# A hybrid decoder layer on one core: 1/rms multiplications two per pooled tile, output-weight pieces in the attention branch, low parts of merged tiles two behind

## The chip, the cores and the metric

The kernel runs on one core of a Trainium2 chip. The metric is the device time of one execution in microseconds, the median of the runs taken; lower is better. Five engines work side by side, each through its own queue in program order: TensorE (PE in the profile; its weight loads are PEld), VectorE (DVE), ScalarE (ACT), GpSimd (POOL) and SyncE (SP), which here only issues transfers. They wait for each other through semaphores.

## The reference

A layer for 256 tokens of width 1024: two token mixers side by side, gated and summed, then a gated feed-forward part with a short convolution. Everything is float32.

```python
h = rmsnorm(x, norm_mix_g)
q, k, v, u_pool, gate_logits = split(h @ w_in)
attn = moba_attention(rope(rmsnorm(q)), rope(rmsnorm(k)), v)      # 8 heads of 64, one causal block
pooled = multiscale_pool_mixer(u_pool, w_pool, pool_scale)        # trailing means of 2, 4, 8, 16
gates = sigmoid(gate_logits + b_gate)                             # two branches of 1024
mixed = gates[0] * (attn @ w_branch_attn) + gates[1] * (pooled @ w_branch_pool)
x = x + mixed @ w_out
h2 = rmsnorm(x, norm_ffn_g)
gate, val = split(causal_depthwise_conv(h2 @ w_up, conv_w, conv_b))
return x + (silu(gate) * val) @ w_down
```

## The kernel before

Activations lie with features on the 128 partitions and the 256 tokens along the free axis, so a feature tile is 128x256. Every float32 product is made of three matmuls (`mm3`, lines 99 to 105): each operand is split into a rounded high part (`high`, line 91, on ScalarE) and the rest as a low part (`low`, line 95 or 97, on VectorE), and high x high, high x low and low x high are summed in PSUM. TensorE takes three matmuls of 256 columns for each 128x128 block of weights.

Weights come in chunks of 128x2048 floats in the order of `order` (line 108): q, k, v, pool inputs, gates, pool maps, two chunks `bp` (pooled branch), two `ba` (attention branch), four `o` (output), then up and down chunks. Each passes four stages: a load on SP into one of four raw buffers, a high part on ScalarE and a low part on VectorE, in two pieces of 1024 columns each, and its use by TensorE. The splitting runs ahead of the use: every call of `ahead()` (line 199) takes the next high piece and the next low piece in order. Three rules limit it. The low piece lags one behind the high one (`STAGGER`). A high piece is not begun while its chunk is four or more ahead of the oldest chunk in use (`WBUFS`); that call then does nothing for it. When a chunk's last low piece is issued, `loads()` issues the load of the chunk four later into the raw buffer that it frees. So the place of an `ahead()` call in the program sets the place of one 128x1024 operation in the queue of ScalarE and one in that of VectorE, and of a load in SP's.

Every engine keeps its program order; the last lines (933 to 939) tie each instruction to the one before it on its engine.

The stage that the change touches has two loops of eight tiles, each tile twelve matmuls into one of four PSUM banks of the pool `mm`.

The pooled branch (lines 721 to 740): tile j of the pooled map, evacuated by a multiplication with its sigmoid gate (line 738; line 728 for tiles 4 and 5, where the attention values of all heads are also multiplied out in PSUM, weighed on VectorE at line 644, and split into the tiles `heads`). Six attention gates were copied out of PSUM earlier without their factor 1/rms (`plain`, line 704); they get it here (line 740), one a tile in tiles 0 to 5. ScalarE takes one sigmoid a tile (`sigmoids`, line 656), of the attention gates from tile 2 on. There is one `ahead()` in each tile.

The attention branch (lines 746 to 758): tile j is evacuated by a multiplication with its gate (line 753, VectorE), GpSimd adds the gated pooled tile (line 754), ScalarE rounds the sum to `mh` (line 755), VectorE makes the rest `ml` (line 757). The low part of tile j − 1 is issued in tile j, that of tile 7 behind the loop. `ahead()` is called in tiles 1 and 3 and behind the loop.

The output stage (lines 797 to 810) multiplies `mh` and `ml` with the output weights. For its first chunk it takes inputs 0 to 6 of its first tile, 0 to 6 of its second, and then input 7 of both.

Of the kernel before, what the change touches and what calls it, by code (L numbers as in the profile page):

```python
# [10 lines left out]
ALU = mybir.AluOpType  # L11
# [6 lines left out]
KD = D // P  # L18
# [38 lines left out]
VALUES = 4  # L57
# [13 lines left out]
def hybrid_layer_kernel(ctx: ExitStack, tc: tile.TileContext, xq_d, xtok_d, par_d, wkv_d, wpg_d,  # L71
                        wpool_d, wba_d, wbp_d, wout_d, wup_d, wdn_d, out_d):
    nc = tc.nc
# [16 lines left out]
    def high(hi, src, scale=1.0):  # L90
        nc.scalar.activation(hi, src, AF.Copy, scale=scale)  # L91

    def low(lo, hi, src, scale=None):
        if scale is None:
            nc.vector.tensor_tensor(lo, src, hi.bitcast(F32), ALU.subtract)  # L95
        else:
            nc.vector.scalar_tensor_tensor(lo, src, scale, hi.bitcast(F32), ALU.mult, ALU.subtract)
# [66 lines left out]
    def next_high():  # L164
        if at[0] < len(pieces):
            c, sl, first, _ = pieces[at[0]]
            if c - oldest() >= WBUFS:
                return
            at[0] += 1
            if first:  # L170
                moving = order[c][0] in "qkv"
                place = MOVING if moving else 0
                his[c] = whi_p.tile([P, CH + P], F32R, tag="whi", name=f"hi_{order[c][0]}{c}")[:, place:]
                place = MOVING if moving else FAR
                los[c] = wlo_p.tile([P, CH + P], F32R, tag="wlo", name=f"lo_{order[c][0]}{c}")[:, place:]
            high(his[c][:, sl], raw(c, sl))

    def next_low(eager=False):
        if at[1] < at[0] - STAGGER or at[0] == len(pieces) > at[1] or (at[1] < at[0] and eager):
            c, sl, _, last = pieces[at[1]]  # L180
            at[1] += 1
            low(los[c][:, sl], his[c][:, sl], raw(c, sl))
            if last:
                split.add(c)
                loads()
# [13 lines left out]
    def ahead(upto=0):  # L199

        next_high()
        next_low()
        if at[1] - sum(p[0] < used[0] for p in pieces) < upto:
            next_high()
            next_low()

    def chunk(name):
        c = used[0]
        used[0] += 1
        spent.update(i for i in range(c) if order[i][0] != "dn")  # L210
        assert order[c][0] == name and all(p[0] != c or name == "dn" and p[3] for p in pieces[at[1]:]), (name, order[c][0])
        return his[c], los[c]
# [63 lines left out]
    R1 = const.tile([P, S], F32, name="R1")  # L276
# [158 lines left out]
    def tick():  # L435
        clock[0] += 1
        for fn, args in due.pop(clock[0], []):
            fn(*args)
# [80 lines left out]
    def gate(n):  # L519
        return gates[:, n // 2, n % 2, :]  # L520
# [96 lines left out]
    def values(hps):  # L617

        po = ps2.tile([P, 2, 512], F32, tag="ps2", name=f"ps_o{hps[0]}")
        for i, hp in enumerate(hps):  # L620
            for b in range(2):
                for j in range(2):
                    h = 2 * hp + j
                    out = po[j * DH:(j + 1) * DH, i, 0:S].rearrange("p (a t r) -> p a t r", a=4, r=32)
                    nc.tensor.matmul(out[:, :, b:2, :], vn[:, b, h * DH:(h + 1) * DH],
                                     soft[hp][:, :, 3 * j + 2 * b:3 * j + b + 2, :], start=b == 0, stop=b == 1)
        return po
# [10 lines left out]
    def rounded(hps, po):  # L638
        if not heads:
            both = act.tile([P, 2, KA, S], F32R, tag="at", name="heads")  # L640
            heads.extend(both[:, i] for i in range(2))
        for i, hp in enumerate(hps):
            v = weighed(hp)
            nc.vector.tensor_tensor(v, po[:, i, 0:S].rearrange("p (a t r) -> p a t r", a=4, r=32), v, ALU.mult)
            high(tokens(heads[0], hp), natural(hp))

    def rests(hps):
        for hp in hps:
            low(tokens(heads[1], hp), tokens(heads[0], hp), natural(hp))
# [3 lines left out]
    def sigmoids(n):  # L653
        for _ in range(min(n, len(waiting))):
            f = waiting.pop(0)
            nc.scalar.activation(gate(f), gate(f), AF.Sigmoid, bias=par[:, C_BG + f:C_BG + f + 1])
# [19 lines left out]
    plain = []  # L676
    for n in range(2 * KD):
# [23 lines left out]
        f = 2 * GATES[b] + c  # L701
# [11 lines left out]
    def branch(src, oph, opl, j, w):  # L713
        hi, lo = w
        ps = bank(f"ps_b{src}{j}")
        for k in range(4):
            sl = slice(k * 512 + (j % 4) * P, k * 512 + (j % 4 + 1) * P)
            mm3(ps[:, 0:S], (hi[:, sl], lo[:, sl]), (oph[:, k, :], opl[:, k, :]), k == 0, k == 3)
        return ps

    for j in range(KD):
        if j % 4 == 0:
            w = chunk("bp")
        ps = branch("p", poolh, pooll, j, w)
        if j == VALUES:
            pos = [(hps, values(hps)) for hps in ((0, 1), (2, 3))]
        if j in (VALUES, VALUES + 1):
            nc.vector.tensor_tensor(gate(KD + j), ps[:, 0:S], gate(KD + j), ALU.mult)
            for hps, po in pos:
                rounded(hps, po) if j == VALUES else rests(hps)  # L730
        if j % 2 == 1:
            tick()
            ahead()
        if j in (0, 2, 4, 6):
            ahead()
        sigmoids(1)
        if j not in (VALUES, VALUES + 1):
            nc.vector.tensor_tensor(gate(KD + j), ps[:, 0:S], gate(KD + j), ALU.mult)
        if j < len(plain):
            nc.vector.tensor_tensor(gate(plain[j]), gate(plain[j]), R1, ALU.mult)  # L740
    mixer.close()
    tmp = ctx.enter_context(tc.tile_pool(name="ffn", bufs=2))
    mh = act.tile([P, KD, S], F32R, tag="qk", name="mh")
    ml = act.tile([P, KD, S], F32R, tag="v", name="ml")
    pend = []
    for j in range(KD):
        if j % 4 == 0:
            w = chunk("ba")
        ps = branch("a", heads[0], heads[1], j, w)
        sigmoids(1)  # L750
        if j in (1, 3):
            ahead()
        nc.vector.tensor_tensor(gate(j), ps[:, 0:S], gate(j), ALU.mult)
        nc.gpsimd.tensor_tensor(gate(j), gate(j), gate(KD + j), ALU.add)
        high(mh[:, j, :], gate(j))
        if j:
            low(ml[:, j - 1, :], mh[:, j - 1, :], gate(j - 1))
    low(ml[:, KD - 1, :], mh[:, KD - 1, :], gate(KD - 1))
    ahead()


# [243 lines left out]
```

## Time and profile before

| | us |
|---|---|
| median of 3 runs | 329.03 |
| lowest, highest | 328.9, 333.66 |
| profiled execution | 328.88 |
| its span, first to last instruction | 327.1 |
| mean granted TensorE clock | 1.00 |

The span was also cut into stages. Each row below is one stretch, in us from the span's start, with its length, each engine's busy time and (in brackets) instructions, the granted clock, the DMA share and GB/s. The first is the end of the gates, the second the pooled branch with the attention values, the third the attention branch, the fourth and fifth the output stage.

```profile
92.00:97.00 5.00, 5.00 (x47) 5.00 (x46) 4.26 (x6) 4.97 (x9) 0.00 (x0) 1.00 1.08 282
97.00:111.00 14.00, 14.00 (x132) 13.12 (x131) 11.61 (x25) 9.24 (x18) 0.00 (x0) 1.00 0.98 341
111.00:122.00 11.00, 11.00 (x99) 11.00 (x98) 8.68 (x18) 5.56 (x11) 5.11 (x6) 1.00 0.45 177
122.00:133.50 11.50, 11.50 (x104) 11.50 (x103) 8.29 (x14) 8.18 (x13) 2.67 (x4) 1.00 0.38 135
133.50:144.50 11.00, 11.00 (x100) 11.00 (x99) 8.51 (x14) 7.24 (x13) 3.10 (x4) 1.00 0.60 235
```

The order of the columns is PE, PEld, DVE, ACT, POOL. A timeline row gives the start and the duration in us, the engine, the line of the program, the operation and its output and inputs by the program's names (`xq` holds the gates as well as the input); in square brackets stands the idle time of the engine ahead of it and what ended that. A duration runs to the end of the pipeline: the next instruction of the same engine can start a little before it. A matmul record lasts 0.28 us although the next one starts after 0.113.

### The profile page before, as it was taken

To read this page: it belongs to the slowest core of one execution; us is meant where nothing else is said; L and a number is where in the kernel's file an instruction comes from. 1 tells how busy PE (TensorE), PEld (TensorE's weight loads), DVE (VectorE), ACT (ScalarE), POOL (GpSimd) and SP (SyncE) were. 2 spreads that over 40 slices of the span, in tenths; PEclk is the share of its full clock that TensorE was granted. 3 is DMA by queue.
4 is the path that set the end of the run, shared out by engine and by line. 5 is a ranking of instruction groups with operands and counts; after the bars stand their busy time and mean duration, and the time that the engine had idled before them with its cause. 6 is when DMAs were issued, how large, how long until landed. Compare 5 with 4: busy or idle time off the path is not lost.

```text
span 327.1 us, 6769 instructions
## 1 busy us (share of the span) xinstructions
PE 322.7 (99%) x2708; PEld 316.1 (97%) x2708; DVE 259.3 (79%) x447; ACT 201.8 (62%) x329; POOL 71.5 (22%) x89
## 2 busy tenths in 40 slices
PE   8999999999999999999999999999999999999995
PEld 8888899999999999999999999999999999999995
DVE  4839989999988966879997978686868686868834
ACT  5768518675994657669675647474747474746520
POOL 1006690000000151230421221212121212121330
PEclk9999999999999999999999999999999999999999
DMA  7999799947799833635527455464646464643003
GB/s 263 420 415 236 200 373 299 310 141 280 260 284 336 318 128 127 254 137 178 208 100 288 178 208 212 174 217 172 217 169 215 172 219 167 222 164 130 0 2 128
DMA packets 16542, 69.72 MB, mean 213 GB/s; under 512 B 2176, under 2 KB 7040, under 8 KB 9856
## 3 DMA queue, kind: packets, MB, share of 16 engines
q1 hardware_dynamic: 16096, 69.17, 60.1%
q8 instruction: 21, 0.34, 0.4%
q10 hardware_dynamic: 416, 0.13, 0.2%
q14 instruction: 9, 0.07, 0.1%
HBM read 65.61 MB, written 3.69 MB: 212 GB/s over the span
## 4 chain that ended last, share of the span: by engine, by line
PE 99%; DVE 0%; issue 0%
PE ps_up L105 12%; PE ps_up L103 12%; PE ps_up L104 12%; PE ps_d L867 6%; PE ps_d L865 6%; PE ps_d L866 6%; PE ps_g L103 5%; PE ps_g L105 4%; PE ps_g L104 4%; PE ps_q L333 4%; PE ps_k L333 3%; PE ps_v L333 3%; PE ps_out L103 2%; PE ps_out L105 2%; PE ps_out L104 2%; PE ps_warm L248 1%
## 5 line engine op out<-in xcount | busy, mean ns | idle before, releaser
L105 PE MATMUL ps_up<-hhi,lo_up 128*128 128x256 f32 x352 | 97.2, 276 | 0.0
L103 PE MATMUL ps_up<-hhi,hi_up 128*128 128x256 f32 x352 | 97.2, 276 | 0.0
L104 PE MATMUL ps_up<-hlo,hi_up 128*128 128x256 f32 x352 | 97.2, 276 | 0.0
L104 PEld LDWEIGHTS ps_up<-hlo,hi_up 128*128 128x128 f32 x352 | 66.1, 188 | 0.0
L105 PEld LDWEIGHTS ps_up<-hhi,lo_up 128*128 128x128 f32 x352 | 66.1, 188 | 0.0
L103 PEld LDWEIGHTS ps_up<-hhi,hi_up 128*128 128x128 f32 x352 | 66.1, 188 | 0.0
L95 DVE TENSOR_TENSOR lo_up<-raw_up,hi_up 128x1024 fp32r<-128x1024 f32 x44 | 54.7, 1261 | 7.3 <-ACT hi_up L91 7.3
L865 PE MATMUL ps_d<-ah,hi_dn 128*128 128x256 f32 x176 | 48.6, 276 | 0.0
L866 PE MATMUL ps_d<-al,hi_dn 128*128 128x256 f32 x176 | 48.6, 276 | 0.0
L867 PE MATMUL ps_d<-ah,lo_dn 128*128 128x256 f32 x176 | 48.6, 276 | 0.0
L91 ACT ACTIVATE hi_up<-raw_up 128x1024 fp32r<-128x1024 f32 x44 | 44.1, 1046 | 0.0
L847 POOL TENSOR_TENSOR c_v<-c_g,c_v 128x256 f32<-128x256 f32 x22 | 16.3, 739 | 121.4 <-DVE c_v L830 121.4
L91 ACT ACTIVATE ah<-c_v 128x256 fp32r<-128x256 f32 x22 | 9.2, 418 | 45.6 <-POOL c_v L847 45.6
L103 PE MATMUL ps_g<-xhi,hi_g 128*128 128x256 f32 x128 | 35.6, 278 | 0.0
L105 PE MATMUL ps_g<-xhi,lo_g 128*128 128x256 f32 x128 | 35.4, 276 | 0.0
L104 PE MATMUL ps_g<-xlo,hi_g 128*128 128x256 f32 x128 | 35.4, 276 | 0.0
L865 PEld LDWEIGHTS ps_d<-ah,hi_dn 128*128 128x128 f32 x176 | 33.0, 188 | 0.0
L866 PEld LDWEIGHTS ps_d<-al,hi_dn 128*128 128x128 f32 x176 | 33.0, 188 | 0.0
L867 PEld LDWEIGHTS ps_d<-ah,lo_dn 128*128 128x128 f32 x176 | 33.0, 188 | 0.0
L95 DVE TENSOR_TENSOR lo_dn<-raw_dn,hi_dn 128x1024 fp32r<-128x1024 f32 x22 | 27.8, 1263 | 0.4 <-ACT hi_dn L91 0.4
L835 DVE TENSOR_TENSOR u_v<-ps_up,R 128x256 f32<-128x256 f32 x22 | 9.3, 421 | 20.9 <-PE ps_up L105 20.8
L872 POOL TENSOR_TENSOR al<-c_v,ah 128x256 fp32r<-128x256 f32 x22 | 22.0, 1002 | 11.6 <-ACT ah L91 11.6
(197 smaller groups left out, 780.9 us busy)
## 6 DMA issues: line engine op xcount, KB each, us to landing
raw_up<-in_wup SPq DMA_DIRECT2D x22, 1024.0 KB, 4.9
raw_g<-in_wpg SPq DMA_DIRECT2D x8, 1024.0 KB, 8.4
raw_dn<-in_wdn SPq DMA_DIRECT2D x8, 1024.0 KB, 4.9
raw_o<-in_wout SPq DMA_DIRECT2D x4, 1024.0 KB, 10.6
raw_dn<-in_wdn SPq DMA_DIRECT2D x6, 512.0 KB, 4.9
raw_v<-in_wkv SPq DMA_DIRECT2D x2, 1024.0 KB, 15.5
raw_p<-in_wpg SPq DMA_DIRECT2D x2, 1024.0 KB, 13.1
raw_bp<-in_wbp SPq DMA_DIRECT2D x2, 1024.0 KB, 5.4
```

Of the source, the lines that this page charges most:

```text
L91: nc.scalar.activation(hi, src, AF.Copy, scale=scale)
L95: nc.vector.tensor_tensor(lo, src, hi.bitcast(F32), ALU.subtract)
L103: nc.tensor.matmul(out, sh, mh, start=start, stop=False, **kw)
L104: nc.tensor.matmul(out, sh, ml, start=False, stop=False, **kw)
L105: nc.tensor.matmul(out, sl, mh, start=False, stop=stop, **kw)
L333: nc.tensor.matmul(pt[t][:, c:c + wide], sx[:, k, t * P:(t + 1) * P], wx[:, sl], start=k == 0 and c == 0 and sx is xhi and wx is hi, stop= ...
L835: nc.vector.tensor_tensor(u, ps[:, 0:S], R2, ALU.mult)
L847: nc.gpsimd.tensor_tensor(uc[1], g[1], uc[1], ALU.mult)
L865: nc.tensor.matmul(o, hi[:, sl], acch[i], start=first, stop=False, skip_group_check=True)
L866: nc.tensor.matmul(o, hi[:, sl], accl[i], start=False, stop=False, skip_group_check=True)
L867: nc.tensor.matmul(o, lo[:, sl], acch[i], start=False, stop=i == KF - 1, skip_group_check=True)
L872: nc.gpsimd.tensor_tensor(accl[i], act_i, acch[i].bitcast(F32), ALU.subtract)
```

## The change

Three edits in the two loops.

- Pooled branch: the 1/rms factors of `plain` are applied two a tile in tiles 0, 1 and 2 instead of one a tile in tiles 0 to 5.
- Weight pieces: `ahead()` is called in pooled tiles 0 to 3 only (before: in all eight), and in attention tiles 1, 2, 4 and 6 (before: 1 and 3). The call behind the attention loop stays.
- Attention branch: the low part of tile j − 2 is issued in tile j, and those of tiles 6 and 7 behind the loop.

No operation is added or removed; the same operations stand at other places of the queues.

```diff
         if j % 2 == 1:
             tick()
-            ahead()
-        if j in (0, 2, 4, 6):
+        if j < VALUES:
             ahead()
         sigmoids(1)
         if j not in (VALUES, VALUES + 1):
             nc.vector.tensor_tensor(gate(KD + j), ps[:, 0:S], gate(KD + j), ALU.mult)
-        if j < len(plain):
-            nc.vector.tensor_tensor(gate(plain[j]), gate(plain[j]), R1, ALU.mult)
+        for f in plain[2 * j:2 * j + 2]:
+            nc.vector.tensor_tensor(gate(f), gate(f), R1, ALU.mult)
...
         ps = branch("a", heads[0], heads[1], j, w)
         sigmoids(1)
-        if j in (1, 3):
+        if j in (1, 2, 4, 6):
             ahead()
         nc.vector.tensor_tensor(gate(j), ps[:, 0:S], gate(j), ALU.mult)
         nc.gpsimd.tensor_tensor(gate(j), gate(j), gate(KD + j), ALU.add)
         high(mh[:, j, :], gate(j))
-        if j:
-            low(ml[:, j - 1, :], mh[:, j - 1, :], gate(j - 1))
-    low(ml[:, KD - 1, :], mh[:, KD - 1, :], gate(KD - 1))
+        if j > 1:
+            low(ml[:, j - 2, :], mh[:, j - 2, :], gate(j - 2))
+    for j in (KD - 2, KD - 1):
+        low(ml[:, j, :], mh[:, j, :], gate(j))
     ahead()
```

`VALUES` is 4.

## The prediction

> **What bounds the kernel now.** I read the page's busy shares and chain first, then what TensorE waited for.
>
> ```profile
> PE 322.7 (99%) x2708; PEld 316.1 (97%) x2708; DVE 259.3 (79%) x447; ACT 201.8 (62%) x329; POOL 71.5 (22%) x89
> ...
> PE 99%; DVE 0%; issue 0%
> ```
>
> ```profile
> PE ps_warm L248 <- DVE ones L216: 1.1, 1, 1.1
> ```
>
> The chain that ends last is TensorE at 99%, and the view of waits has one wait of TensorE in the whole run, 1.1 us at the start. So nothing on another engine holds it up in the stages that are changed: an edit that frees VectorE, ScalarE or POOL there can win nothing, and one that delays them costs only what exceeds their slack. The forecast is therefore a question of slack, and slack is read from two timelines, TensorE first: the last matmul of attention tile 0, matmuls of the first output tile, and the last matmul of that tile.
>
> ```profile
> 112.39 0.28 PE L105 MATMUL ps_ba<-heads,lo_ba 128*128 128x256 f32 x1
> ...
> 122.02 0.28 PE L103 MATMUL ps_out<-mh,hi_o 128*128 128x256 f32 x1
> 122.14 0.28 PE L104 MATMUL ps_out<-ml,hi_o 128*128 128x256 f32 x1
> ...
> 123.50 0.28 PE L104 MATMUL ps_out<-ml,hi_o 128*128 128x256 f32 x1
> ...
> 124.18 0.28 PE L104 MATMUL ps_out<-ml,hi_o 128*128 128x256 f32 x1
> ...
> 127.01 0.28 PE L105 MATMUL ps_out<-mh,lo_o 128*128 128x256 f32 x1
> ```
>
> A matmul starts every 0.113 us, so one attention tile (12 of them) takes 1.36 us, and the low part of merged tile k is read at 122.14 + 0.34 k: k = 4 at 123.50, k = 6 at 124.18 (k = 7 comes only after the second tile's seven, at about 126.9). VectorE makes those parts:
>
> ```profile
> 113.01 0.42 DVE L753 TENSOR_TENSOR xq<-ps_ba,xq 128x256 f32<-128x256 f32 x1
> 113.34 1.22 DVE L95 TENSOR_TENSOR lo_o<-raw_o,hi_o 128x1024 fp32r<-128x1024 f32 x1
> 114.48 0.42 DVE L753 TENSOR_TENSOR xq<-ps_ba,xq 128x256 f32<-128x256 f32 x1
> 115.64 0.49 DVE L95 TENSOR_TENSOR ml<-xq,mh 128x256 fp32r<-128x256 f32 x1 [0.74 <-ACT mh L91]
> 116.06 0.41 DVE L753 TENSOR_TENSOR xq<-ps_ba,xq 128x256 f32<-128x256 f32 x1
> ...
> 123.60 0.41 DVE L95 TENSOR_TENSOR ml<-xq,mh 128x256 fp32r<-128x256 f32 x1
> ...
> 127.32 0.42 DVE L776 TENSOR_TENSOR xq<-ps_out,xq 128x256 f32<-128x256 f32 x1 [0.66 <-PE ps_out L105]
> ```
>
> The low part of tile 6 ends at 123.60 + 0.41 = 124.01 and is read at 124.18. The slack of the whole attention stage is 0.17 us. That is the number on which the change is to be judged.
>
> **Prices.** The rows above and these give them.
>
> ```profile
> 115.19 0.42 ACT L91 ACTIVATE mh<-xq 128x256 fp32r<-128x256 f32 x1 [1.81 <-POOL xq L754]
> 115.52 0.50 ACT L656 ACTIVATE xq<-xq,par 128x256 f32<-128x256 f32 x1
> 115.92 1.04 ACT L91 ACTIVATE hi_o<-raw_o 128x1024 fp32r<-128x1024 f32 x1
> 116.87 0.40 ACT L91 ACTIVATE mh<-xq 128x256 fp32r<-128x256 f32 x1
> ```
>
> ```profile
> 113.51 1.65 POOL L754 TENSOR_TENSOR xq<-xq 128x256 f32<-128x256 f32 x1 [63.89 <-DVE xq L753]
> 116.55 0.74 POOL L754 TENSOR_TENSOR xq<-xq 128x256 f32<-128x256 f32 x1 [0.69 <-DVE xq L753]
> ```
>
> From start to next start: a 256-wide operation on VectorE 0.33, a weight piece there 1.14; on ScalarE a merged tile's high part 0.33, a sigmoid 0.40, a weight piece 0.95. An evacuation starts 0.31 after its last matmul starts (127.01 to 127.32). POOL starts 0.08 after the evacuation's end; ScalarE and VectorE follow within 0.03.
>
> POOL's add takes 0.74 alone, but 1.65 when it starts (113.51) inside the weight piece of 113.34: it lasts until that piece gives way at 114.48 and then 0.68 more. The opposite holds too:
>
> ```profile
> 160.84 0.73 POOL L847 TENSOR_TENSOR c_v<-c_g,c_v 128x256 f32<-128x256 f32 x1 [1.89 <-DVE c_v L830]
> ```
>
> ```profile
> 160.95 1.71 DVE L95 TENSOR_TENSOR lo_dn<-raw_dn,hi_dn 128x1024 fp32r<-128x1024 f32 x1
> ```
>
> ```profile
> 131.46 1.22 DVE L95 TENSOR_TENSOR lo_o<-raw_o,hi_o 128x1024 fp32r<-128x1024 f32 x1
> 132.59 0.97 DVE L97 SCALAR_TENSOR_TENSOR hlo<-xq,par,hhi 128x256 fp32r<-128x256 f32 x1
> ```
>
> ```profile
> 132.53 0.75 POOL L785 TENSOR_TENSOR ss<-ss,s 128x256 f32<-128x256 f32 x1 [7.91 <-ACT s L783]
> ```
>
> A piece that starts inside a POOL operation takes 1.71 instead of 1.22: it runs only from about 0.13 before POOL's end. At 132.5 POOL came in between two such VectorE operations, and the second took 0.97. So VectorE operations with two SBUF inputs (pieces, low parts, not evacuations from PSUM) and POOL's adds take turns. I hold that rule in both directions.
>
> [...]
>
> **The change, part by part.**
>
> 1. The six 1/rms multiplications (0.33 each), two a tile over three tiles instead of one over six.
>
> ```profile
> 102.27 1.23 DVE L95 TENSOR_TENSOR lo_ba<-raw_ba,hi_ba 128x1024 fp32r<-128x1024 f32 x1 [0.73 <-ACT hi_ba L91]
> ...
> 104.74 0.42 DVE L728 TENSOR_TENSOR xq<-ps_bp,xq 128x256 f32<-128x256 f32 x1
> 105.76 0.42 DVE L644 TENSOR_TENSOR RS<-ps_o,RS 128x256 f32<-128x256 f32 x1 [0.60 <-PE ps_o L625]
> ```
>
> Two of the three that move ahead of 102.27 fall into its 0.73 us of idling; the rest stand in the same stretch up to tile 3. Tile 4's evacuation stays at 104.74. Cost 0. The sigmoid that waited 1.1 us for the last of them waits no more; that wait held no tensor work: gain 0.
>
> ```profile
> L656 ACT ACTIVATE xq<-xq,par 128x256 f32<-128x256 f32 x16 | 7.3, 495 | 1.1 <-DVE xq L740 1.1
> ```
>
> 2. The aheads of pooled tiles 4 to 7 go, attention tiles 1 and 3 become 1, 2, 4 and 6. Two of the removed calls did nothing (the four-buffer limit on chunks stopped them), so four weight pieces move, each 0.95 on ScalarE and 1.14 on VectorE: low pieces from pooled tiles 4 and 5 and attention tiles 1 and 3 to attention tiles 1, 2, 4 and 6. The planner's state after the last ahead is the same, so nothing changes in kind from the output stage on. With 2.3 us less in front of it, VectorE keeps up with TensorE, and attention tile 0 is evacuated when ready, at 112.39 + 0.31 = 112.70 (113.01 before).
>
> Loads on SP: the last output chunk's load waits for the moved low piece of the attention weights, the first up chunk's for output chunk 0.
>
> ```profile
> 108.98 0.33 SPq L135 DMA_DIRECT2D raw_o<-in_wout  x1
> ```
>
> ```profile
> 114.59 0.33 SPq L135 DMA_DIRECT2D raw_up<-in_wup  x1
> ```
>
> ```profile
> 126.73 0.33 SPq L135 DMA_DIRECT2D raw_up<-in_wup  x1
> ```
>
> ```profile
> DMA to landing us min/median/max: 5.6/10.6/11.9
> ```
>
> ```profile
> 128.50 2.00 ACT L91 ACTIVATE hi_o<-raw_o 128x1024 fp32r<-128x1024 f32 x2
> ```
>
> They move to about 114.3 and 121.2; the second up chunk's, behind the stage's last piece, from 126.7 to 128.5. With the slowest landing, 11.9, the output chunk is there at 126.2; its first reader is the second of the two at 128.50, 129.45 before. Cost 0; the SP queue holds only further weight loads behind them.
>
> 3. Low parts two tiles behind. By itself it lets VectorE wait less for the high part of the tile just merged. In the stage below it is worth about nothing: the low parts are late because their add and high part are late.
>
> **The sum.** I follow the queues in program order with the prices above; an operation starts when its queue is free and its input is there. The same rules on the old order put the end of low part 6 at 124.04; the trace has 124.01.
>
> At tile 1 the new order has on ScalarE: high 0, sigmoid, first output piece, high 1; on VectorE: attention piece at once behind evacuation 0. That piece (113.04 to 114.17) makes add 0 end at 114.85, as before. But now the first output piece is on ScalarE behind high 0 and the sigmoid: 114.88 + 0.33 + 0.40 = 115.61, done 116.66, and its low half, which VectorE reaches at 114.50, stands ahead of evacuation 2. VectorE idles 2.2 us there and evacuation 2 comes at 117.83 instead of 116.06. From then on VectorE is never ahead, and low parts, pieces and adds take turns:
>
> ```
> tile  evacuation  add ends  high ends  low ends  read at   shift of TensorE
>  1      114.17     115.55    116.98     119.47    122.48    0
>  2      117.83     119.18    119.63     121.82    122.82    0
>  3      118.50     120.06    120.51     122.70    123.16    0
>  4      121.07     122.41    122.86     125.06    123.50    1.6
>  5      121.73     123.30    123.75     125.94    123.84    2.1
>  6      124.30     125.65    126.10     126.83    124.18    2.7
>  7      124.97     126.54    126.99     127.44    126.90    2.7
> ```
>
> The piece of tile 4 is reached at 119.38, but add 3 holds it to 119.93; that of tile 6 is reached at 122.62 and held by add 5 to 123.17: two waits of 0.55 each, on VectorE, with evacuations 4 and 6 queued behind. The shift is low end + 0.03 − read time, never shrinking. No PSUM bank is late: tile 6 on TensorE begins at 119.30 and needs evacuation 2, done 118.25. Nothing after the stage wins the shift back, since TensorE has no other wait; what follows is paced by it.
>
> The sum is 0 + 0 + 2.7 = 2.7 us on top of the profiled execution, 328.9 us (span 327.1), which is 0.1 below the median of three, 329.03: 331.6 us.
>
> Bounds: from below the stall can be 0, as the row of waits shows now; it is no gain, since TensorE waits for nothing to be removed. From above, with VectorE held to POOL's full end, 3.5. I take 2.7, because the rules give the old stage to 0.03 us.
>
> **Rivals.**
>
> *Hidden anyway: not slower.* If POOL and VectorE did not hold each other up, the same order ends low part 6 at 123.99 and TensorE never waits: 328.9 to 329.1 us. For it: 0.17 us of slack would then be enough. Against it: 1.65 and 1.71. Chance 0.12.
>
> *Only POOL waits, VectorE does not.* Low part 6 ends at 125.02, shift 0.9: 329.8. Against it: 1.71 and 0.97. Chance 0.10.
>
> *Full block:* VectorE stays held until POOL's recorded end; low part 6 then ends at 127.61, shift 3.5: 332.3. Chance 0.12; against it, that the 1.71 is 0.49 over 1.22 and not 0.62.
>
> *The late output chunk:* its load starts 5.3 us later, and its high piece holds ScalarE's queue. It decides only from a landing of 17.9 us on (114.3 to 129.45 + 2.7); each further microsecond costs one, so over 2% needs some 22 us, where the slowest of these loads took 11.9. Chance 0.03, near 336.
>
> **Numbers.** Forecast 0.60 at 331.6 (its own range 331.0 to 332.2); the rivals 0.12, 0.10, 0.12 and 0.03; 0.03 for what I did not think of. Range 329.4 to 332.7: it leaves out the hidden case and the late chunk. Two per cent is 6.6 us, about what a measurement of this kernel can tell from no change; only the late chunk and the unforeseen reach it: faster 0.01, same 0.95, slower 0.04.
>
> **What would show it.** TensorE waits for low parts of tiles 4, 5 and 6 (ps_out on ml), some 2.7 us in three pieces near 123.5, and nowhere else; VectorE idles about 2.2 us near 114.5 on the high output piece; evacuations 4 and 6 near 121.1 and 124.3; the pieces of tiles 4 and 6 last about 1.8 us. It is wrong if TensorE shows no wait at ps_out, or if it waits in the attention tiles themselves (a bank), or for a raw chunk.

## The result, and the profile after

| | before | changed |
|---|---|---|
| median, us | 328.96 | 331.73 |
| lowest, highest of 20 runs each | 328.45, 333.66 | 331.15, 333.42 |
| profiled execution, its span | 328.88, 327.1 | 332.94, 331.2 |
| granted clock of the profiled execution | 1.000 | 0.995 |

The changed kernel takes 1.0091 times as long (95% interval 1.0077 to 1.0106). The medians lie 2.8 us apart; 331.6 us were predicted, and 331.73 came. The page's busy shares and chain, and the view of TensorE's waits:

```profile
PE 324.8 (98%) x2708; PEld 317.3 (96%) x2708; DVE 260.9 (79%) x447; ACT 201.6 (61%) x329; POOL 71.8 (22%) x89
...
PE 94%; DVE 3%; POOL 1%; ACT 1%; issue 0%; POOLq 0%
```

```profile
PE ps_out L104 <- DVE ml L95: 1.9, 3, 1.4
```

VectorE, POOL and ScalarE now stand in the chain that ends last, and TensorE has one new kind of wait: three times for a low part of the merged tiles. Its timeline (start, duration, and in brackets the wait) shows the three places:

```profile
123.04 0.28 PE L103 MATMUL ps_out<-mh,hi_o 128*128 128x256 f32 x1
124.75 0.39 PE L104 MATMUL ps_out<-ml,hi_o 128*128 128x256 f32 x1 [1.44 <-DVE ml L95]
124.98 0.28 PE L105 MATMUL ps_out<-mh,lo_o 128*128 128x256 f32 x1
125.09 0.28 PE L103 MATMUL ps_out<-mh,hi_o 128*128 128x256 f32 x1
125.62 0.39 PE L104 MATMUL ps_out<-ml,hi_o 128*128 128x256 f32 x1 [0.25 <-DVE ml L95]
...
126.50 0.39 PE L104 MATMUL ps_out<-ml,hi_o 128*128 128x256 f32 x1 [0.25 <-DVE ml L95]
```

A matmul starts 0.113 us after the one before it when nothing is missing (122.93 to 123.04). 123.04 to 124.75 is 1.71, a pause of 1.60; the next two are 0.42 each. The matmul behind each pause starts 0.22 or 0.23 us later (124.75 to 124.98) in place of 0.113: a restart costs 0.11 here. Three pauses and three restarts are 2.77 us. (The bracket counts from the modelled end of the matmul before, so it shows less.)

VectorE's timeline of the same stretch; the changed kernel's lines 752 and 753 are the evacuation and the add:

```profile
112.36 0.42 DVE L752 TENSOR_TENSOR xq<-ps_ba,xq 128x256 f32<-128x256 f32 x1 [0.86 <-PE ps_ba L105]
112.70 1.22 DVE L95 TENSOR_TENSOR lo_ba<-raw_ba,hi_ba 128x1024 fp32r<-128x1024 f32 x1
113.83 0.42 DVE L752 TENSOR_TENSOR xq<-ps_ba,xq 128x256 f32<-128x256 f32 x1
116.35 1.23 DVE L95 TENSOR_TENSOR lo_o<-raw_o,hi_o 128x1024 fp32r<-128x1024 f32 x1 [2.10 <-ACT hi_o L91]
117.49 0.42 DVE L752 TENSOR_TENSOR xq<-ps_ba,xq 128x256 f32<-128x256 f32 x1
...
119.05 1.76 DVE L95 TENSOR_TENSOR lo_o<-raw_o,hi_o 128x1024 fp32r<-128x1024 f32 x1
120.73 0.41 DVE L752 TENSOR_TENSOR xq<-ps_ba,xq 128x256 f32<-128x256 f32 x1
...
122.28 1.75 DVE L95 TENSOR_TENSOR lo_o<-raw_o,hi_o 128x1024 fp32r<-128x1024 f32 x1
123.96 0.41 DVE L752 TENSOR_TENSOR xq<-ps_ba,xq 128x256 f32<-128x256 f32 x1
...
125.77 0.68 DVE L95 TENSOR_TENSOR ml<-xq,mh 128x256 fp32r<-128x256 f32 x1 [0.20 <-ACT mh L91]
```

VectorE stands idle for 2.10 us on the high half of the first output piece, and two weight pieces that start inside an add of POOL take 1.76 and 1.75 instead of the 1.22 of the piece at 112.70. The adds, two in each row:

```profile
117.99 1.74 POOL L753 TENSOR_TENSOR xq<-xq 128x256 f32<-128x256 f32 x2 [2.78 <-DVE xq L752]
121.28 1.68 POOL L753 TENSOR_TENSOR xq<-xq 128x256 f32<-128x256 f32 x2 [1.55 <-ACT hi_o L91]
```

The first pair ends at 119.73, and the piece that started at 119.05 ends 1.08 us after that, so it ran only from about 0.14 before the adds' end. This execution runs 0.34 us ahead of the old one at the start of the stage (112.36 for the predicted 112.70); with that taken off, evacuations 2, 4 and 6 were predicted for 117.49, 120.73 and 123.96.

The profiled execution is 4.1 us longer than the old one, not 2.8. The rest is the clock (1.6 us), less the 0.34 us by which this execution was ahead: 2.77 + 1.6 - 0.34 = 4.0. The view by windows (PE, PEld, DVE, ACT, POOL busy, then the granted clock) has, directly behind the pauses:

```profile
127.20:130.60 3.40, 3.40 (x18) 3.40 (x17) 1.01 (x1) 1.85 (x3) 0.00 (x0) 0.51 0.34 84
130.60:134.00 3.40, 3.40 (x32) 3.40 (x31) 1.89 (x3) 2.13 (x4) 0.00 (x0) 1.00 0.55 231
```

For 3.4 us TensorE ran at half its clock: 16 matmuls started 0.10 us later each than they should, 1.6 us in all. Seven of the 20 runs show a granted clock of 0.994 or 0.995, and they take 332.9 to 333.4 us; the other 13, at 0.999 or 1.000, take 331.2 to 332.2. The median of those 13 is 331.58 us, 2.6 above the kernel before; that the medians of all runs differ by just the 2.77 us of the trace is chance.

### The profile page after: what moved, and what is told of

Read it like the earlier page. It is cut to its first block, busy times and chain, and to the rows that moved or that the text cites. A ratio compares the mean times of both kernels' runs of the same rounds, so it can differ in the third digit from the quotient of the medians.

```text
span 331.2 us, 6770 instructions
## 1 busy us (share of the span) xinstructions
PE 324.8 (98%) x2708; PEld 317.3 (96%) x2708; DVE 260.9 (79%) x447; ACT 201.6 (61%) x329; POOL 71.8 (22%) x89
## 4 chain that ended last, share of the span: by engine, by line
PE 94%; DVE 3%; POOL 1%; ACT 1%; issue 0%; POOLq 0%
PE ps_up L104 12%; PE ps_up L103 12%; PE ps_up L105 12%; PE ps_d L866 6%; PE ps_d L865 6%; PE ps_d L867 6%; PE ps_g L103 4%; PE ps_g L105 4%; PE ps_g L104 4%; PE ps_q L333 3%; PE ps_k L333 3%; PE ps_v L333 3%; PE ps_out L104 2%; PE ps_out L105 2%; PE ps_out L103 2%; DVE lo_o L95 1%
```

## The experiments

The theory is the prediction's: the four weight pieces make the low parts late, by two things together, the order on ScalarE (the first output piece behind the high part of tile 0) and the turns of VectorE and POOL. Its rivals put the delay on one of the other edits, or on one of the two things alone.

### One part at a time

**e1**: the multiplications alone.

```diff
-        if j < len(plain):
-            nc.vector.tensor_tensor(gate(plain[j]), gate(plain[j]), R1, ALU.mult)
+        for f in plain[2 * j:2 * j + 2]:
+            nc.vector.tensor_tensor(gate(f), gate(f), R1, ALU.mult)
```

> Only the 1/rms multiplications two a tile, the rest as before. Theory (the moved pieces make the whole delay): no wait of TensorE in the output stage, 329.0 us, the same as before within 0.3. Rival (the multiplications push the evacuation of pooled tile 4 and all behind it): that evacuation later than 104.7 relative to the old order by up to 1.0 us, and a wait of TensorE at the attention or output tiles, 329.3 to 330.

Measured: 328.78 us against 328.77, ratio 0.9997 (0.9975 to 1.0018). TensorE's only wait is the one at the start.

```profile
105.13 0.42 DVE L728 TENSOR_TENSOR xq<-ps_bp,xq 128x256 f32<-128x256 f32 x1
```

```profile
101.55 1.06 ACT L91 ACTIVATE hi_ba<-raw_ba 128x1024 fp32r<-128x1024 f32 x1 [2.60 <-DMA raw_ba<-in_wba]
```

And in the kernel before:

```profile
101.17 1.06 ACT L91 ACTIVATE hi_ba<-raw_ba 128x1024 fp32r<-128x1024 f32 x1 [2.37 <-DMA raw_ba<-in_wba]
```

The evacuation of pooled tile 4 comes 0.39 us later than 104.74, but so does the landing of the weights that VectorE waits for ahead of it (101.55 against 101.17 on ScalarE). The multiplications add nothing.

**e2**: the moved pieces alone.

```diff
             tick()
-            ahead()
-        if j in (0, 2, 4, 6):
+        if j < VALUES:
             ahead()
...
-        if j in (1, 3):
+        if j in (1, 2, 4, 6):
             ahead()
```

> Only the four weight pieces moved into attention tiles 1, 2, 4 and 6; multiplications as before, low parts one tile behind. Theory: the pieces alone make the delay; by the same queue rules low parts 5 and 6 end 1.5 and 2.8 us late, so TensorE waits at ps_out for ml twice or three times, 2.8 us in all, 331.6 to 332 us. Rival (the low parts two behind are what is late): no wait, 329.0 us. In runs with a granted clock below 1.000 some 1.6 us more.

Measured: 331.64 us against 328.77, ratio 1.0087 (1.0058 to 1.0115), two of six runs at clock 0.995. The whole loss is in this part. The waits are not quite those expected: TensorE pauses three times (1.34, 0.70 and 0.41 us), and the second pause is for a high part, that of tile 6, not for a low one. TensorE's waits, and VectorE's timeline at the low parts of tiles 2 and 4:

```profile
PE ps_out L104 <- DVE ml L95: 1.2, 1, 1.2
...
PE ps_out L103 <- ACT mh L91: 0.5, 1, 0.5
```

```profile
119.82 0.49 DVE L95 TENSOR_TENSOR ml<-xq,mh 128x256 fp32r<-128x256 f32 x1 [0.75 <-ACT mh L91]
...
123.20 0.50 DVE L95 TENSOR_TENSOR ml<-xq,mh 128x256 fp32r<-128x256 f32 x1 [0.75 <-ACT mh L91]
```

With the low parts one tile behind, VectorE waits 0.75 us for each of those high parts (and for that of tile 6) and no piece is caught in an add; with them two behind it does not wait there, and its pieces run into the adds instead. Both come to nearly the same time, 2.87 and 2.77 us above the kernel before, by two different waits. The account by ScalarE's order and the turns together is therefore that of the changed kernel; in e2 POOL's adds come in pairs, and every pair but the first (2.35 us) takes 1.46 to 1.54.

**e3**: the low parts two behind, alone.

```diff
-        if j:
-            low(ml[:, j - 1, :], mh[:, j - 1, :], gate(j - 1))
-    low(ml[:, KD - 1, :], mh[:, KD - 1, :], gate(KD - 1))
+        if j > 1:
+            low(ml[:, j - 2, :], mh[:, j - 2, :], gate(j - 2))
+    for j in (KD - 2, KD - 1):
+        low(ml[:, j, :], mh[:, j, :], gate(j))
```

> Only the low parts of merged tiles two tiles behind; multiplications and pieces as before. Theory: low part 6 ends at about 123.9 against 124.0 before, no wait of TensorE, 329.0 us. Rival (the later low parts use up the 0.17 us of slack): a wait of TensorE for ml of 0.2 to 0.9 us, 329.2 to 330.

Measured: 328.84 us against 328.77, ratio 1.0005 (0.9979 to 1.0030), no wait of TensorE but the first. The old slack of 0.17 us is not used up.

### The two causes, each taken away

**e5**: the high pieces stay where they were on ScalarE; only the low pieces move.

```diff
         if j < VALUES:
             ahead()
+        if j in (VALUES, VALUES + 1):
+            next_high()
...
-        if j in (1, 2, 4, 6):
-            ahead()
+        if j in (1, 3):
+            next_high()
+        if j in (1, 2, 4, 6):
+            next_low()
```

> The changed kernel, but the four high pieces on ScalarE stay at their old places (pooled tiles 4 and 5, attention tiles 1 and 3); only the low pieces on VectorE are moved. Theory: of the 2.8 us the part that comes from the first output piece standing on ScalarE behind the high part of tile 0 goes away (VectorE does not idle 2.1 us at attention tile 1), the part from VectorE and GpSimd taking turns stays: by the same queue rules a wait of TensorE for ml of 0.9 us, 329.8 to 330.1 us. Rival (the turns alone make the delay, ScalarE's order does not matter): the wait stays above 2 us, 331.3 us or more. Rival (ScalarE's order alone): no wait, 329.0.

Measured: 330.08 us against 329.26; the ratio, 1.0009 (0.9986 to 1.0032), does not separate them (the 23 runs of the kernel before go from 328.84 to 332.2 here), so the trace has to. It shows two pauses of 0.38 and 0.41 us with a restart each, 1.0 us.

```profile
114.59 1.43 DVE L95 TENSOR_TENSOR lo_o<-raw_o,hi_o 128x1024 fp32r<-128x1024 f32 x1
...
117.71 1.76 DVE L95 TENSOR_TENSOR lo_o<-raw_o,hi_o 128x1024 fp32r<-128x1024 f32 x1
...
120.94 1.75 DVE L95 TENSOR_TENSOR lo_o<-raw_o,hi_o 128x1024 fp32r<-128x1024 f32 x1
```

The first output piece starts at 114.59 with no wait ahead of it, and the idle 2.1 us are gone; the pieces are stretched by the adds as before. ScalarE's order carries 1.75 of the 2.77 us when the turns are there, and the turns keep 1.0 when it is put right.

**e4 and e9**: POOL's step writes and does not read.

```diff
-        nc.gpsimd.tensor_tensor(gate(j), gate(j), gate(KD + j), ALU.add)
+        for _ in range(3):
+            nc.gpsimd.memset(gate(j), 0.5)
```

> The changed kernel, but GpSimd's add of the pooled branch is replaced by three fills of the same tile (each about 0.31 us, together about as long as an add alone, 0.87 against 0.74), in the same place of the same chain of waits; the sum of the two branches is left out. The fills read nothing. Theory (VectorE operations with two SBUF inputs and GpSimd operations that read SBUF take turns): with nothing read the turns are gone, all weight pieces last 1.22 us, the GpSimd operations are not stretched, low part 6 ends near 124.3, the wait of TensorE is 0 to 0.3 us, 329.0 to 329.3 us. Rival (no turns, or turns whatever GpSimd does; the order on ScalarE and the length of the GpSimd step make the delay): the wait stays at 2 us or more, 331 us or more; with turns against any GpSimd operation 3.6 us, 332.5.

Measured with three fills: 329.58 us against 328.77, ratio 1.0016 (1.0001 to 1.0030), a little above the 329.0 to 329.3 expected. POOL's step took 1.05 us, not the 0.87 that I had worked out, and two pauses of 0.3 us each are left, with restarts 0.8 in all. No VectorE piece is stretched. To have the step no longer than an add, the same with two:

> As the run with three fills, with two: GpSimd's step is then about 0.68 us (three took 1.05), a little shorter than the add alone (0.74), and reads nothing; the sum of the two branches is left out, everything else is the changed kernel. Theory (turns): VectorE's pieces last 1.22, low part 6 ends near 124.0, no wait of TensorE or one under 0.1 us, 329.0 us, the same as before. Rival (the order on ScalarE makes the delay by itself): a wait of 1.7 us or more, since that order is not changed here.

Measured: 329.18 us against 329.24, ratio 0.9988 (0.9969 to 1.0006), no wait of TensorE but the first.

```profile
115.50 1.23 DVE L95 TENSOR_TENSOR lo_o<-raw_o,hi_o 128x1024 fp32r<-128x1024 f32 x1 [1.11 <-ACT hi_o L91]
...
117.97 1.22 DVE L95 TENSOR_TENSOR lo_o<-raw_o,hi_o 128x1024 fp32r<-128x1024 f32 x1
```

```profile
117.11 1.35 POOL L754 MEMSET xq<- 128x256 f32 x4 [1.99 <-DVE xq L752]
```

POOL's four fills at 117.11 overlap a low part and the piece of 117.97, and nobody waits: 1.35 for four, 1.22 for the piece. The step is 0.68 us, 0.06 shorter than an add alone, and the whole 2.77 us are gone. VectorE still waits 1.11 us on ScalarE's order, and that alone costs nothing. The 0.06 us do not make the difference, by an estimate from the two runs: low part 6 came 0.68 us too late with a step of 1.05 and 0.23 us early enough with one of 0.68, so 0.06 us are worth about 0.15, less than the 0.23 left. In these rows a piece takes 1.22 beside fills, which read nothing, and 1.76 beside adds, which read two tiles in SBUF.

**e10**: the add on VectorE.

```diff
-        nc.gpsimd.tensor_tensor(gate(j), gate(j), gate(KD + j), ALU.add)
+        nc.vector.tensor_tensor(gate(j), gate(j), gate(KD + j), ALU.add)
```

> The changed kernel with the add of the pooled branch on VectorE instead of GpSimd, right behind the evacuation that it needs. The turns are gone and the high parts come earlier, but VectorE has eight adds more, each 0.33 us and 0.12 us of waiting for the evacuation in front of it. Theory: VectorE itself is then the bound of the stage; the queue rules give a wait of TensorE of 1.8 us (three pauses), up to 2.5 with the dependent starts, so 331.0 to 331.8 us, no gain worth the name on the changed kernel. Rival (GpSimd's step is the whole trouble): no wait, 329.0 us.

Measured: 330.96 us against 329.24, ratio 1.0051 (1.0027 to 1.0076). Two pauses of 1.18 and 0.67 us, not three; no piece is stretched, and VectorE is busy with next to no gap.

```profile
120.02 0.42 DVE L752 TENSOR_TENSOR xq<-ps_ba,xq 128x256 f32<-128x256 f32 x1
120.47 0.43 DVE L753 TENSOR_TENSOR xq<-xq 128x256 f32<-128x256 f32 x1
120.81 0.42 DVE L95 TENSOR_TENSOR ml<-xq,mh 128x256 fp32r<-128x256 f32 x1
```

An add behind its own evacuation starts 0.45 us after it instead of 0.33. The turns are gone, but the VectorE time that replaces them costs nearly as much: the two pauses and their restarts come to 2.1 us, against 2.77.

### The clock

One pause in the old kernel, made by extra VectorE work ahead of low part 6, n = 4, 8 and 12:

```diff
+        if j == KD - 1:
+            scr = tmp.tile([P, S], F32, tag="scr", bufs=1, name="scr")
+            for _ in range(n):
+                nc.vector.tensor_tensor(scr, ps[:, 0:S], gate(KD + j), ALU.mult)
         if j:
             low(ml[:, j - 1, :], mh[:, j - 1, :], gate(j - 1))
```

> The kernel before with four extra VectorE multiplications (PSUM and SBUF input, 0.33 us each, into a tile nobody reads) ahead of the low part of merged tile 6: one pause of TensorE of 1.2 us, once. Theory on the clock (it falls when a stretch of about 3.4 us holds too little work): granted clock 1.000 in every run, and 1.2 + 0.1 us for the restart on top of before, 330.1 us.

> The same with eight extra multiplications: one pause of 2.5 us, as much idle time as the three pauses of the changed kernel have together. Theory: 331.4 us in the runs at clock 1.000 and, as with the changed kernel, a part of the runs (a third or so) at 0.995 and 1.6 us longer. Rival (it is the several restarts that make the clock fall): no run below 1.000, all at 331.4.

> The same with twelve: one pause of 3.9 us. Theory: nearly every run has its clock halved for about 3.4 us, so 328.8 + 3.9 + 0.1 + 1.6 = 334.4 us and a clock of 0.995. Rival (the clock falls by chance, whatever the pause): a third of the runs or fewer, median 332.8.

Measured: 331.56, 334.60 and 337.88 us against 329.26; ratios 1.0051 (1.0020 to 1.0081), 1.0135 (1.0084 to 1.0186), 1.0226 (1.0173 to 1.0279). The extra multiplications of e6 took 0.45 us each, not 0.33 (an estimate from the row of the four, 1.78 us, with 0.42 for the last). Each writes the tile of the one before; that it waits for it is an estimate from e10, where an add behind its own evacuation starts 0.45 us after it. The pauses are 1.6, 3.4 and 5.6 us and all three times missed what was expected. The profiled execution of e8 has two shorter pauses besides, 0.91 and 0.41 us, one of them in the attention branch. One run of e6 was at low clock, where none was expected. The runs still bear on the question they were made for, when the clock falls. The theory given for e6 counts the work over a stretch of about 3.4 us; no run shows such a count, and what the trace of the changed kernel shows is one fall that lasts 3.41 us. Pauses are read from the gaps between matmul starts in the profiled execution, low clock is 0.995 or less:

| kernel | idle in all, us | longest pause | runs at low clock |
|---|---|---|---|
| e4 | 0.6 | 0.35 | 0 of 12 |
| e5 | 0.80 | 0.41 | 0 of 12 |
| e6 | 1.60 | 1.60 | 1 of 12 |
| e10 | 1.84 | 1.18 | 2 of 12 |
| e2 | 2.4 | 1.34 | 2 of 6 |
| changed kernel | 2.44 | 1.60 | 7 of 20 |
| e7 | 3.4 | 3.4 | 4 of 6 |
| e8 | 6.9 | 5.6 | 6 of 6 |

The longer TensorE idles, the more runs are at low clock, from 0 of 12 at 0.80 us to 6 of 6 at 6.9. In the trace of the changed kernel that costs 1.6 us, at a mean clock of 0.995; two of e7's runs and five of e8's stand at 0.990. A single pause does it (e7, 3.4 us, 4 of 6 runs), so several restarts are not needed for it.

## Why the prediction was right, point by point

- *TensorE bound, slack 0.17 us.* Right: apart from the clock, nothing but the stage's lateness changed the time, and e1 and e3, which stay inside the slack, cost nothing.
- *Part 1, multiplications: 0.* Right (e1), with a miscount that changes nothing: two multiplications, not three, move ahead of the piece at 102.27 (tiles 0 and 1 hold four in place of two), and two of 0.33 fit into its 0.73 us. In the profiled execution of the changed kernel the evacuation of pooled tile 4 stands at 107.42, not 104.74, because the attention weights' second chunk had landed later; it held up nothing.
- *Part 2, weight pieces: 2.7.* Right in place, order and size. Predicted pauses 1.59, 0.54 and 0.55 (low end + 0.03 − read time, each less the one before); measured 1.60, 0.42 and 0.42 with 0.11 for the restart behind each. The restarts behind the first two fall into the next wait, so the total differs only by the last one: 2.77. The three loads came at 113.99, 120.84 and 128.27 (predicted 114.3, 121.2, 128.5, less the 0.34), and no matmul waited for a weight chunk.
- *Part 3, two behind: nothing.* Right in size in both settings: e3 against the kernel before, and the changed kernel (2.77 above its kernel before) against e2 (2.87). With the moved pieces it is an exchange, though, which the prediction did not say: the waits of 0.75 us for high parts go, and pieces caught in adds come in their place.
- *The rule of turns, in both directions.* Right: the rows show both directions, and in e9, with fills in place of the adds, no piece is stretched (1.22) and the loss is gone (329.18 us against 329.24). The prediction counted two waits of 0.55 on VectorE; the rows have 1.76 and 1.75 against 1.22, and for POOL 1.65 against 0.74 (its add at 113.51 in the kernel before). The rivals "hidden" (0), "only POOL waits" (0.9) and "full block" (3.5) are out: 2.77. No run shows VectorE held to POOL's recorded end, as the 3.5 has it; the piece of 119.05 ran from about 0.14 us before that end.
- *What it did not have:* the clock. It said that what follows the stage is paced by TensorE and keeps the shift; in 7 of 20 runs the shift grew by 1.6 us. Had those been the majority, 333 us would have stood outside the range given. Nothing in the prediction says why they were not, so that much of the hit is luck. It also held two per cent for about the least that can be told from no change; the interval here is 0.3 per cent wide.

One thing reads differently now. The sum laid the 2.7 us out as one chain, and it is tempting to share it between its two causes. They do not add: with the turns removed the order on ScalarE costs nothing (e9), with the order put right the turns cost 1.0 (e5), and together they cost 2.77.

No version here beats the kernel before. In it TensorE already waits for nothing after the first microsecond, and all that these kernels change is whether that stays so.

## What to carry to other kernels

When one engine is never idle, moving work about on the others can win nothing and can cost; find the smallest slack of the stage that receives it (here 0.17 us, one subtraction of two timeline rows) before adding to it. A step that is split over two queues is as late as its later half: a piece moved into a chain of four engines must be followed on each of them, in program order. In these traces weight pieces on VectorE and adds on POOL, both with two SBUF inputs, held each other up: a piece that started inside an add took 1.76 in place of 1.22 us, and an add that started inside a piece 1.65 in place of 0.74. An evacuation from PSUM inside an add kept its 0.42 (118.16 in the changed kernel), and a piece beside fills its 1.22 (e9). So such pieces and adds should not be interleaved where a chain runs through both.

## What was not expected of the hardware

TensorE's granted clock fell to a half for 3.4 us after pauses that were each well under that length: 1.6 us at most in the changed kernel.

```profile
127.23 0.42 PE L103 MATMUL ps_out<-mh,hi_o 128*128 128x256 f32 x1
127.45 0.42 PE L104 MATMUL ps_out<-ml,hi_o 128*128 128x256 f32 x1
```

There a matmul starts every 0.21 us and lasts 0.42 in place of 0.113 and 0.28. In the table above idle time of less than 3.4 us was enough: with 2.44 us in three pieces 7 of 20 runs fell, with one pause of 1.6 us 1 of 12.

The traces of the two kernels give the times at which the granted clock changes. In the changed kernel it rises to full at 4.26 us (matmuls start every 0.21 us ahead of it, every 0.11 or 0.12 behind it), falls to a half at 127.14 and rises again at 130.55; in the kernel before it rises at 6.07 and next falls at 326.92, at the end of the run. These distances, 122.88, 3.41 and 320.85 us, are 36, 1 and 94 times 3.413. The last 3.41 us ahead of the fall at 127.14 hold 1.87 us of idle time of TensorE: 1.03 of the first pause, and the two of 0.42.

The sum of the idle time alone does not tell which execution falls. The profiled executions of e6 (one pause of 1.60 us), of e10 (1.18 and 0.67) and of e2 (1.34, 0.70 and 0.41, 2.4 in all) ran at 1.000, 0.999 and 1.000; that of the changed kernel (1.60 and twice 0.42, 2.44 in all) ran at 0.995, that of e7 (3.4) at 0.995 and that of e8 (6.9) at 0.990. Nor do all runs of one kernel agree: 7 of 20 ran at 0.994 or 0.995. What decides between nearly equal idle times is not shown.
